# A norm factor computed two value groups sooner, and three weight splits moved behind a bank's read, in a two-layer hybrid decoder step on one Trainium2 core

## The chip, the core and the metric

The kernel runs on one core of a Trainium2 chip. Five engines work side by side, each through its own queue, in order: TensorE (PE; its weight loads are shown apart as PEld), VectorE (DVE), ScalarE (ACT), GpSimd (POOL) and SyncE (SP), which here issues all DMA transfers. An instruction that has to wait for another engine holds up everything behind it on its own engine. The metric is the device time of one execution in microseconds (us).

## The reference

There are 1088 tokens: 1024 of a prompt and 8 x 8 sample tokens. Layer 0 is a gated linear attention with 4 heads, layer 1 a token-mixing MLP on chunks of 128 positions. Cut to what the change touches:

```python
def gla_mixer(h, s0, w_in, ...):            # h = rmsnorm(x, norm_g[0])
    q, k, v, gate, a_low = split(h @ w_in)
    q = q * GLA_DK ** -0.5
    log_a = log_sigmoid(a_low @ w_a_up + b_a_up) / 16
    o, s_new = gla_chunked(q, k, v, log_a, s0, 64)
    return (rmsnorm(o, g_onorm) * silu(gate)) @ w_out, s_new

def cmlp_mixer(h, w_in, ...):               # h = rmsnorm(x, norm_g[1])
    u, v, gate = split(h @ w_in, 3)
    v = layernorm(v, ln_g, ln_b)
    mixed = einsum('gts,bnsgd->bntgd', tril(w_spatial), v) + b_spatial
    return (u * mixed * silu(gate)) @ w_out, v
```

## The kernel before

**Number format.** Matmuls run on operands split into a high part (the value rounded to the fast matmul format, a copy on ACT) and a low part (value minus high part, a subtraction on DVE). Each product is then three matmuls: high x high, high x low, low x high. So every weight tile that arrives costs one ACT and one DVE instruction before PE can use it: `fetch_w` (L127, L128) in most stages and `parts_of` (L972, L973) in the u/gate stage. Each tile here is 128 x 512 values.

**Start of layer 0.** The tokens lie in three pieces of 384, 384 and 320. The norm is applied late: matmuls run on x times the norm's gain, and the factor 1/rms of each token (`rs[p]`) is multiplied in when a result is read out. `squares_x(p)` sums x*x over the eight row blocks (ACT squares L236, DVE adds L238). `rstd_x(p)` sums over the partitions with a matmul of ones (L244, tile ssq) and makes the factor in two ACT steps (L179 logarithm, L181 exponential) and four DVE steps (L180, L182, L183, L184). `evac_qk` reads the queries and keys of a piece out of PSUM times that factor (L264, L266). `token_rstd` sends the factors through memory to lay them out by token (L190, L191, L194, tile rtm).

Queries and keys of head 0 are multiplied first, for all three pieces; the third piece's wait in two PSUM banks (tile third) for their factor. Then come the groups of values of head 0, `v_group(0, i)`, i = 0 to 8, one per 128 tokens, 24 matmuls each (L156), with 16 extra columns: the input of the forget gate (tile alt). Groups 0 to 4 (`AHEAD` = 5) run ahead of the attention's work. After group 3 (`LOW0` = 3) stand `a_low(0)`, which transposes the gate inputs of the first piece (L252) and splits them (L255, L256, L257), and `gates()` of the first piece: one matmul (L419), then L422 to L426 and a scan (L428) that gives the running sum of the log gates, cum. From cum come the attention's operands: `borders` (L435 to L449) and `level_prep` (L459 to L463, L470 to L483), on DVE, ACT and POOL, for the matmuls of `level` (L509, L518).

**What sets the order there.** Outside the u/gate stage, a planner orders the instructions of each engine when the kernel is built: it goes through them by its own estimate of when each is ready, and among those that are ready the earlier line of the program goes first. Moving a line changes its rank, and can change the order of others. The tiles' buffers are few: the tag misc, from which ssq, pa and z (the banks of the norm, the gate inputs and the gate matmul) come, has two PSUM banks.

**u/gate stage of layer 1.** From L1006 to L1267 the order is that of the program (`in_order`). The stage computes, for each of m = 0 to 7, 128 columns of u and of gate for all tokens. The 2 x 2 blocks of weights and tokens are combined so that seven products do the work of eight: the weights appear plain, (1,1), (1,2), (2,2), and as sums s1 to s4 made on POOL (`sums`, L985) out of the raw quarters (`Quarters`: four loads of 256 KB, L964, into one buffer, rawq). `parts(key, place)` splits one of them into a place (L972, L973); a place is free once the products that used the previous weights in it are done. `nxt` holds the weights of m + 1, `following` the loads for m + 2.

One m runs through products in this order, each for two halves r of 272 columns, 12 matmuls a half (L1004): s2 into the banks pb, s3 into two, s1 on pb, (1,1) into p, then the token mixing (L1106), s4 on pb, (2,2) on two, (1,2) on p. Between them: L1139 and L1179 copy halves out on ACT, L1165 adds pb to sg on DVE, L1191 and L1192 add halves on POOL, L1210 multiplies the norm factor on DVE and L1211 is the SiLU on ACT; L1218 reads pb for the last time on DVE, after which the next m's s2 product may write that bank; L1220 and L1222 multiply on POOL; L1240 reads two for the last time on DVE. `v_load(m + 1)` (L1076, L1077) loads the next values for mixing, normalised by L1083 on ACT.

For m = 0 the splits for m = 1 have an order of their own, since nothing was ready earlier. The lines are:

```python
for key, at in (((1, 1), "s2"), ((2, 2), "s3"), ((1, 2), "s1")):   # L1207
    nxt.parts(key, w[at])
following = Quarters(22)
V.tensor_tensor(sg[:, fb], sg[:, fb], rs_all[:, fb], ALU.mult)     # L1210
A.activation(sg[:, fb], sg[:, fb], AF.Silu)                        # L1211
nxt.parts("s2", spare)                                             # L1213
for r in R:
    product(pb[r], w["s4"], b22[r], start=False)                   # L1217
    V.tensor_tensor(p1[r], p1[r], pb[r], ALU.add)                  # L1218
    if r == 0:
        G.tensor_tensor(zt[:, qb[r]], zt[:, qb[r]], p1[r], ALU.mult)
```

Of the kernel before, what the change touches and what calls it, by code (L numbers as in the profile page):

```python
# [34 lines left out]
WARM, AHEAD, LOW0 = 9, 5, 3  # L35
# [5 lines left out]
def trunk_kernel(ctx: ExitStack, tc: tile.TileContext, a: dict):  # L41
# [28 lines left out]
    def ps(tag, name, bufs=2):  # L70
        return pp.tile([P, 512], F32, tag=tag, bufs=bufs, name=name)
# [114 lines left out]
    def token_rstd(p):  # L186

        t0, n, nch = PIECES[p]
        row = a["r_spill"]
        SP.dma_start(row[:, t0:t0 + n], rs[p][0:1, :])  # L190
        SP.dma_start(rtm[:, 3 * p:3 * p + nch], row[0, t0:t0 + nch * P].rearrange("(c q) -> q c", q=P))  # L191
        if p == 2:
            for r in (0, NS):
                SP.dma_start(rtm[r:r + NS, 8:9], row[0, SEQ:T].rearrange("(c q) -> q c", q=NS))  # L194
# [20 lines left out]
    def gq(tag, name, bufs):  # L215
        return gc.tile([P, NPMAX], F32, tag=tag, bufs=bufs, name=name)
# [24 lines left out]
    def rstd_x(p, acc, ms, t):  # L241
        n = size[p]
        ssq = ps("misc", "ssq")[:, :n]
        PE.matmul(ssq, ones, acc, start=True, stop=True)  # L244
        rstd(ssq, D, rs[p], ms[:, :n], t[:, :n])
# [15 lines left out]
    def evac_qk(h, p, j, acc):  # L261
        t = gq("qk"[j], "qk"[j] + f"{h}_{p}", 4)[:, :size[p]]
        if j == 0:
            V.scalar_tensor_tensor(t, acc, QSCALE, rs[p], ALU.mult, ALU.mult)  # L264
        else:
            V.tensor_tensor(t, acc, rs[p], ALU.mult)  # L266
        (q, k)[j][h, p] = t
# [13 lines left out]
    first = [ps("mm", f"first{j}")[:, :size[0]] for j in range(2)]  # L281
# [9 lines left out]
    for i, t in enumerate((lvmask, smask)):  # L291
        f = wp.tile([P, 512], F32, tag="raw", bufs=3, name="mask")[:, :448]
# [24 lines left out]
    third = [fm_block(ws_[0], j * P, h0[2], 2, wide[:, j, :]) for j in range(2)]  # L317
# [7 lines left out]
    acc2 = squares_x(2)  # L325
# [5 lines left out]
    def gt(tag, name, bufs, shape=(P, NPMAX)):  # L331
        into = gc if tag in ("v", "la", "e", "cum", "dec") else gp
        return into.tile(list(shape), F32, tag=tag, bufs=bufs, name=name)
# [405 lines left out]
    ahead = block_groups(1)  # L739
    for i, g in enumerate(ahead[:AHEAD]):  # L740
        g()
        if i == LOW0:
            a_low(0)
            flat[0].gates()
    rstd_x(2, acc2, *(gt("sq", f"sq{j}", 2) for j in range(2)))
    for j in range(2):
        evac_qk(0, 2, j, third[j])
    token_rstd(2)
    hs = side_by_side(h0[2], "hs0", gc)

    LEAD = 3
# [1 line left out]
    for h in range(HEADS):  # L753
# [18 lines left out]
        at = {}  # L772
# [11 lines left out]
    i = 0  # L784
# [224 lines left out]
    nxt = None  # L1009
    for blk in range(16, 20):  # L1010
        cs = slice((blk - 16) * 256, (blk - 15) * 256)
        for j, i in enumerate((4, 5, 6, 7, 8, 0, 1, 2, 3) if blk == 19 else range(9)):
# [24 lines left out]
            if (blk, j) == (18, 7):  # L1037
                nxt = Quarters(20)
# [85 lines left out]
    cur, nxt = nxt, None  # L1124
    for m in range(KT):
        w, g, more = cur.w, m // 2, m + 1 < KT
        first = m == 0
# [12 lines left out]
        if first:  # L1140
            for key in ("s4", (2, 2), (1, 2)):
                cur.parts(key)
            nxt, spare = Quarters(21), place()
# [36 lines left out]
        if mid:  # L1180
            if m + 2 < KT:
                following = Quarters(22 + m)
            else:
                stage = mp.tile([P, 5, N], F32, tag="rawq", name="zstage")
                SP.dma_start(stage, z_d[:, 0:5, 0:N])
                following = None
# [16 lines left out]
            mixed(zt, vm, g, m, bias, 4 * c)  # L1203
        if m == 1:
            nxt.parts("s3", w[1, 1])
        if first:
            for key, at in (((1, 1), "s2"), ((2, 2), "s3"), ((1, 2), "s1")):  # L1207
                nxt.parts(key, w[at])
            following = Quarters(22)
        V.tensor_tensor(sg[:, fb], sg[:, fb], rs_all[:, fb], ALU.mult)  # L1210
        A.activation(sg[:, fb], sg[:, fb], AF.Silu)  # L1211
        if first:
# [3 lines left out]
        for r in R:  # L1216
            product(pb[r], w["s4"], b22[r], start=False)  # L1217
            V.tensor_tensor(p1[r], p1[r], pb[r], ALU.add)  # L1218
            if r == 0:
                G.tensor_tensor(zt[:, qb[r]], zt[:, qb[r]], p1[r], ALU.mult)  # L1220
        mixed(zt, vm, g, m, bias, 0, True)
        G.tensor_tensor(zt[:, qb[1]], zt[:, qb[1]], p1[1], ALU.mult)  # L1222
        V.tensor_tensor(sg[:, fb], sg[:, fb], rs_all[:, fb], ALU.mult)
# [36 lines left out]
        if more:  # L1260
# [3 lines left out]
            cur, nxt = nxt, following  # L1264
# [144 lines left out]
```

## Time and profile before

| | |
|---|---|
| three runs | 935.84, 936.48, 936.76 us (median 936.48) |
| the profiled execution | 939.36 us, of which the span from first to last instruction is 937.6 us |
| busy over the span | PE 96%, PEld 94%, DVE 68%, ACT 49%, POOL 31% |
| mean granted TensorE clock | 0.994 |
| 40 to 60 us (value groups, first gates) | PE busy 18.15 of 20, DVE 13.82 |
| 60 to 80 us (first attention units) | PE busy 17.76 of 20, DVE 19.86 |
| 80 to 100 us | PE busy 20.00 of 20, DVE 14.00 |
| 640 to 660 us (m = 0 of u/gate) | PE busy 20.00 of 20, DVE 12.32, POOL 7.67 |
| 660 to 680 us (end of m = 0, m = 1) | PE busy 18.65 of 20, DVE 17.53, POOL 15.31 |
| 680 to 820 us (the other m) | PE busy 20.00 of every 20 |

How to read it: PE is busy nearly all the time, so a microsecond counts only where PE stands still, and the windows show where that is. In a row of the timeline stand the start, the duration, the engine, the line, the operation, the tiles out<-in, the shape and the count; in brackets the idle time before it and what ended it.

### The profile page before, as it was taken

Reading aid. Unit: us, or ns where it says so; the run is one execution under the profiler, and the core shown is the slowest. Engines: PE = TensorE matmul, PEld = TensorE weight load, DVE = VectorE, ACT = ScalarE, POOL = GpSimd, SP = SyncE. Lnnn points to the kernel's source line nnn. Section 1 sums busy time; section 2 is a strip of 40 time slices with the busy share of each in tenths; the row PEclk is TensorE's granted clock in tenths of the full one; section 3 lists DMA queues with packets and bytes.
Section 4 is the critical chain, followed back from the end, with each engine's and each line's share of the span. In section 5 each row is a group of like instructions: output and inputs, shape, how many; then the busy total and the mean of one; then the engine's idle time right before and its main releaser. Section 6 shows DMA issues by size and latency. Waiting matters only on the chain.

```text
span 937.6 us, 17096 instructions
## 1 busy us (share of the span) xinstructions
PE 904.3 (96%) x6437; PEld 877.5 (94%) x6437; DVE 638.7 (68%) x1288; ACT 461.4 (49%) x980; POOL 287.1 (31%) x307
## 2 busy tenths in 40 slices
PE   8989999999999999989999999999999999999995
PEld 7979989998999989989999999999999999999994
DVE  7888778677875877687653854556877777683246
ACT  7664544444552644554443644457444444465322
POOL 2023332332422332322134110021765555211123
PEclk9999999999999999999999999999999999999998
DMA  9302112301222112423565245554333332464233
GB/s 297 96 1 83 41 45 77 118 29 50 64 77 92 52 35 91 124 74 101 155 226 176 73 145 157 156 171 138 99 126 106 102 97 95 125 222 130 60 109 130
DMA packets 89968, 101.80 MB, mean 109 GB/s; under 512 B 9863, under 2 KB 80845, under 8 KB 89885
## 3 DMA queue, kind: packets, MB, share of 16 engines
q1 hardware_dynamic: 89884, 100.71, 34.4%
q8 instruction: 50, 0.82, 0.4%
q14 instruction: 34, 0.27, 0.1%
HBM read 74.26 MB, written 26.42 MB: 107 GB/s over the span
## 4 chain that ended last, share of the span: by engine, by line
PE 66%; DVE 15%; ACT 5%; DMA 5%; issue 5%; POOL 2%; SPq 1%; DVEq 0%; ACTq 0%; POOLq 0%
PE fm L142 27%; PE tm L156 12%; PE pb L1004 7%; PE two L1004 5%; PE p L1004 4%; DMA xsum<-x_spill 2%; PE sc L518 2%; PE mix L1106 1%; PE pst L589 1%; PE o L628 1%; PE o L597 1%; DVE scT L531 1%; DMA wr<-w 1%; PE o L599 1%; PE tms L172 1%
## 5 line engine op out<-in xcount | busy, mean ns | idle before, releaser
L142 PE MATMUL fm<-act,w 128*128 128x384 f32 (+1 forms) x1632 | 292.3, 334 | 0.5 <-DVE act L203 0.4
L142 PEld LDWEIGHTS fm<-act,w 128*128 128x128 f32 x1632 | 271.1, 189 | 3.2 <-DVE act L206 0.7
L156 PE MATMUL tm<-w,act 128*128 128x256 f32 (+1 forms) x1536 | 193.3, 283 | 1.4 <-ACT vt L1015 1.0
L156 PEld LDWEIGHTS tm<-w,act 128*128 128x128 f32 x1536 | 185.5, 188 | 3.7 <-ACT vt L1015 1.9
L142 PE MATMUL fm<-act,wq 128*128 128x384 f32 (+1 forms) x576 | 97.2, 328 | 1.3 <-ACT wq L127 0.8
L142 PEld LDWEIGHTS fm<-act,wq 128*128 128x128 f32 x576 | 94.7, 188 | 3.4 <-ACT wq L127 1.4
L128 DVE TENSOR_TENSOR w<-wr,w 128x512 fp32r<-128x512 f32 (+1 forms) x80 | 57.2, 732 | 17.4 <-ACT w L127 16.9
L826 POOL TENSOR_TENSOR acc<-acc,sq 128x384 f32<-128x384 f32 (+1 forms) x30 | 30.6, 1023 | 110.8 <-ACT sq L821 110.3
L127 ACT ACTIVATE w<-wr 128x512 fp32r<-128x512 f32 (+1 forms) x80 | 48.7, 625 | 25.2 <-DMA wr<-w 13.7
L848 DVE TENSOR_TENSOR x<-fm,res 128x384 f32<-128x384 f32 (+1 forms) x40 | 21.0, 527 | 50.5 <-PE fm L142 50.5
L1004 PE MATMUL two<-tsum,wq 128*128 128x272 f32 x384 | 51.5, 290 | 0.0
L1004 PE MATMUL pb<-act,wq 128*128 128x272 f32 x384 | 51.4, 290 | 0.0
L821 ACT ACTIVATE sq<-x 128x384 f32<-128x384 f32 (+1 forms) x42 | 21.0, 502 | 61.3 <-DVE x L848 58.3
L1004 PE MATMUL p<-act,wq 128*128 128x272 f32 x384 | 51.0, 289 | 0.0
L1004 PEld LDWEIGHTS p<-act,wq 128*128 128x128 f32 x384 | 49.4, 188 | 0.0
L1004 PEld LDWEIGHTS two<-tsum,wq 128*128 128x128 f32 x384 | 49.2, 189 | 0.0
L1004 PEld LDWEIGHTS pb<-act,wq 128*128 128x128 f32 x384 | 49.1, 189 | 0.0
L473 POOL TENSOR_TENSOR xe<-xe,k 128x384 f32<-128x384 f32 (+2 forms) x24 | 28.7, 1195 | 44.3 <-ACT xe L472 41.1
L659 POOL TENSOR_TENSOR on<-on,g 128x384 f32<-128x384 f32 (+1 forms) x24 | 23.8, 1015 | 57.9 <-DVE on L658 35.1
L449 POOL TENSOR_TENSOR kd<-kd,k 128x384 f32<-128x384 f32 (+1 forms) x12 | 12.0, 1003 | 85.7 <-ACT kd L448 85.7
L480 DVE TENSOR_TENSOR xl<-cum 128x192 f32<-128x192 f32 (+4 forms) x72 | 34.8, 509 | 0.0
L483 DVE TENSOR_TENSOR xl<-xl,q 128x192 f32<-128x192 f32 (+4 forms) x72 | 28.9, 439 | 4.8 <-ACT xl L481 4.8
(265 smaller groups left out, 1638.9 us busy)
## 6 DMA issues: line engine op xcount, KB each, us to landing
wr<-w SPq DMA_DIRECT2D x92, 256.0 KB, 3.1
rawq<-w SPq DMA_DIRECT2D x32, 256.0 KB, 3.6
xsum<-x_spill SPq DMA_DIRECT2D x16, 272.0 KB, 3.2
z_spill<-zt SPq DMA_DIRECT2D x8, 544.0 KB, 2.8
s<-s SPq DMA_DIRECT2D x16, 256.0 KB, 4.3
state_s<-ns SPq DMA_DIRECT2D x32, 128.0 KB, 1.8
v_spill<-vt SPq DMA_DIRECT2D x32, 128.0 KB, 2.5
vm<-v_spill SPq DMA_DIRECT2D x8, 512.0 KB, 4.7
```

The costliest lines, as they stand in the source:

```text
L127: A.activation(w[:, 0], raw, AF.Copy)
L128: V.tensor_tensor(w[:, 1], raw, w[:, 0].bitcast(F32), ALU.subtract)
L142: PE.matmul(acc, lhs, rhs, start=(k == 0), stop=(k == 23))
L156: PE.matmul(acc, lhs, rhs, start=(k == 0), stop=(k == 23))
L473: G.tensor_tensor(xe, xe, kt_[:, :nl], ALU.mult)
L480: V.tensor_tensor(l3[:, :, lo:hi], c3[:, :, (i + 1) * m:], r, ALU.subtract)
L483: V.tensor_tensor(l3[:, :, lo:hi], l3[:, :, lo:hi], q3[:, :, (i + 1) * m:], ALU.mult)
L659: G.tensor_tensor(o, o, gate[h][:, j, t0:t0 + n], ALU.mult)
L821: A.activation(sq, raw[p][:, m, :], AF.Square)
L826: (V if gain is not None and p == 2 or m == KT - 1 else G).tensor_tensor(total, acc[p], sq, ALU.add)
L848: V.tensor_tensor(raw[p][:, m, :], pa, r, ALU.add)
L1004: PE.matmul(acc, lhs, rhs, start=start and k + i == 0, stop=k + i == 5, skip_group_check=not start)
```

## The change

Two places are edited. In the start of layer 0, `rstd_x(2, ...)` moves from behind value group 4 to behind group 2, and the reading out of the third piece's queries and keys and `token_rstd(2)` move from behind group 4 to behind group 3, after the first piece's `gates()`. In the u/gate stage at m = 0, the plain splits (1,1) and (2,2) move from ahead of L1210 to behind the last read of pb's first half and the POOL multiplication of that half; the split (1,2) moves behind the last read of the second half; the loads for m = 2 come after it. No computation is added or removed.

```diff
     for i, g in enumerate(ahead[:AHEAD]):
         g()
+        if i == LOW0 - 1:
+            rstd_x(2, acc2, *(gt("sq", f"sq{j}", 2) for j in range(2)))
         if i == LOW0:
             a_low(0)
             flat[0].gates()
-    rstd_x(2, acc2, *(gt("sq", f"sq{j}", 2) for j in range(2)))
-    for j in range(2):
-        evac_qk(0, 2, j, third[j])
-    token_rstd(2)
+            for j in range(2):
+                evac_qk(0, 2, j, third[j])
+            token_rstd(2)
     hs = side_by_side(h0[2], "hs0", gc)
...
         if m == 1:
             nxt.parts("s3", w[1, 1])
-        if first:
-            for key, at in (((1, 1), "s2"), ((2, 2), "s3"), ((1, 2), "s1")):
-                nxt.parts(key, w[at])
-            following = Quarters(22)
         V.tensor_tensor(sg[:, fb], sg[:, fb], rs_all[:, fb], ALU.mult)
         A.activation(sg[:, fb], sg[:, fb], AF.Silu)
...
             V.tensor_tensor(p1[r], p1[r], pb[r], ALU.add)
             if r == 0:
                 G.tensor_tensor(zt[:, qb[r]], zt[:, qb[r]], p1[r], ALU.mult)
+            if first:
+                for key, at in ((((1, 1), "s2"), ((2, 2), "s3")), (((1, 2), "s1"),))[r]:
+                    nxt.parts(key, w[at])
+        if first:
+            following = Quarters(22)
         mixed(zt, vm, g, m, bias, 0, True)
```

## The prediction

> **What bounds the kernel now.** I read the windows first: the stretch of each edit, and what follows it.
>
> ```profile
> 53.00:79.10 26.10, 22.13 (x157) 19.76 (x155) 25.96 (x61) 16.84 (x40) 10.29 (x11) 1.00 0.04 7
> 79.10:99.90 20.80, 20.75 (x142) 20.27 (x143) 14.85 (x36) 7.87 (x19) 5.06 (x6) 1.00 0.28 86
> 663.20:667.70 4.50, 3.15 (x25) 3.12 (x25) 4.27 (x9) 1.75 (x4) 2.33 (x4) 1.00 0.64 201
> ```
>
> The columns are the stretch, its length, the busy time of PE, PEld, DVE, ACT and POOL, the granted clock, DMA share and GB/s. From 53.0 to 79.1 us DVE is busy 25.96 of 26.10 and PE stands still for 3.97: DVE sets the pace. Behind that PE is full again, so what PE gains in the stretch it keeps. Around 665 us PE loses 1.35 of 4.50. These two places are all that the edits can win.
>
> In the first place DVE's timeline shows it idle just before (start, duration, engine, line, operation, tiles; in brackets the idle time before it):
>
> ```profile
> 44.12 1.68 DVE L238 TENSOR_TENSOR acc<-acc,sq 128x320 f32<-128x320 f32 x3
> 48.09 0.55 DVE L256 TENSOR_TENSOR alow<-pa,alow 16x384 fp32r<-16x384 f32 x1 [2.28 <-ACT alow L255]
> 49.74 0.62 DVE L422 TENSOR_SCALAR la<-z,vecs 128x384 f32<-128x384 f32 x1 [1.11 <-PE z L419]
> 52.48 0.56 DVE L426 TENSOR_TENSOR la<-la,e 128x384 f32<-128x384 f32 x1 [2.12 <-ACT e L425]
> 52.96 0.48 DVE L180 TENSOR_SCALAR sq<-ssq 128x320 f32<-128x320 f32 x1
> 53.36 0.95 DVE L428 TENSOR_TENSOR_SCAN cum<-scan,la 128x384 f32<-128x384 uint8 x1
> ...
> 57.23 0.48 DVE L264 SCALAR_TENSOR_TENSOR q<-third,rs 128x320 f32<-128x320 f32 x1
> 57.63 0.48 DVE L266 TENSOR_TENSOR k<-third,rs 128x320 f32<-128x320 f32 x1
> ```
>
> The squares of the third piece are summed at 45.80 (44.12 + 1.68). Then DVE waits 2.28 + 1.11 + 2.12 = 5.5 us for the chain of the first gates, and only behind it come, among the operations that PE waits for, the six of the third piece: L180, L182, L183, L184, L264, L266.
>
> **The norm edit.** Nothing is added; six DVE, two ACT and two PE instructions move. On DVE each takes 0.40 of its queue (57.23 to 57.63), so 6 x 0.40 = 2.4 us leave the stretch in which DVE is the bound, and they fit into the idle 5.5. What they may delay there, in PE's and ACT's timelines:
>
> ```profile
> 37.24 9.78 PE L156 MATMUL tm<-w,act 128*128 128x272 f32 x76 [0.24 <-DVE w L128]
> ...
> 50.70 0.70 PE L244 MATMUL ssq<-acc,ones_r 128*128 128x320 f32 x2
> ...
> 59.30 0.53 PE L509 MATMUL sc<-x 128*64 128x64 f32 x6 [1.36 <-DVE x L463]
> ```
>
> ```profile
> 52.34 0.52 ACT L179 ACTIVATE sq<-ssq,vecs 128x320 f32<-128x320 f32 x1
> ```
>
> Value group 3 runs at 9.78/76 = 0.129 a matmul, 3.1 us for 24; the row ends at 47.02 with it, so it lies from about 43.8 to 46.9. The sum at 45.8 falls within it. The planner places by its own estimates, which the trace doesn't show; L238 stands in its orders close to where it ran, so I take the ssq matmuls in the middle of group 3, at 45.9. They put the rest back by some 0.3 (2 matmuls of 320 columns instead of 272). Then the ACT logarithm until about 47.1, L180 to 47.7, and L182 to L184 until about 48.9. L256, which would start at 48.09 + 0.3, stands behind these four: another 0.5. So the gate chain is 0.8 late; but L180 no longer stands between L426 and the scan (0.40 back). Net delay 0.4 to 0.5. Queries and keys go into the idle time ahead of L422 or L426 and cost nothing; without that cover, 0.8. Sum: 2.4 - 0.5 = **1.9 us** off at L463, which follows L266 and releases the first scores (59.30, after 1.36 of waiting). PE's 3.97 of standing still is more than 1.9, so PE can take all of it.
>
> Late next is still DVE, with cum's operations. The four DMA issues of `token_rstd` come earlier too, and with them the factors by which value groups 6 to 8 are read out; they pass no other transfer that this stretch waits for (its DMA share is 0.04). Of the two misc banks ssq now takes one ahead of pa and z; z comes after L180 has read it.
>
> Bounds: at worst the six stay on the chain all the same (work is only moved), 0; at best no delay, 2.4. I take 1.9, the row-by-row sum. The planner may order later units differently; the nearest row is the wait at 59.30, 1.36, either way.
>
> **The splits edit.** Here the program's order holds, so each queue can be followed. Before, on POOL and on DVE:
>
> ```profile
> 654.71 1.82 POOL L985 TENSOR_TENSOR qsum<-qsum,rawq 128x512 f32<-128x512 f32 x1
> 656.49 1.22 POOL L1191 TENSOR_TENSOR half<-half 128x272 f32<-128x272 f32 x1
> 657.67 1.22 POOL L1192 TENSOR_TENSOR sg<-sg,half 128x272 f32<-128x272 f32 x1
> 658.85 0.77 POOL L1191 TENSOR_TENSOR half<-half 128x272 f32<-128x272 f32 x1
> 659.59 0.77 POOL L1192 TENSOR_TENSOR sg<-sg,half 128x272 f32<-128x272 f32 x1
> 660.32 1.27 POOL L985 TENSOR_TENSOR qsum<-rawq 128x512 f32<-128x512 f32 x1
> ```
>
> ```profile
> 654.70 3.56 DVE L973 TENSOR_TENSOR wq<-rawq,wq 128x512 fp32r<-128x512 f32 x3
> 660.39 1.79 DVE L1210 TENSOR_TENSOR sg<-sg,rs 128x544 f32<-128x544 f32 x1 [2.13 <-POOL sg L1192]
> 663.43 0.69 DVE L973 TENSOR_TENSOR wq<-qsum,wq 128x512 fp32r<-128x512 f32 x1 [1.25 <-ACT wq L972]
> 664.04 0.78 DVE L1218 TENSOR_TENSOR half<-half,pb 128x272 f32<-128x272 f32 x2
> 664.73 0.28 DVE L1101 SCALAR_TENSOR_TENSOR zt<-mix,lng,bias 128x64 f32<-128x64 f32 x1
> 664.93 0.97 DVE L1223 TENSOR_TENSOR sg<-sg,rs 128x544 f32<-128x544 f32 x1
> 665.82 0.77 DVE L1240 TENSOR_TENSOR sg<-half,two 128x272 f32<-128x272 f32 x2
> 666.52 1.28 DVE L973 TENSOR_TENSOR wq<-qsum,wq 128x512 fp32r<-128x512 f32 x2
> ```
>
> While the three splits run (3.56 instead of about 3 x 0.60, the spacing of 663.43 to 664.04), POOL's additions are long too: 1.82 against 1.27, 1.22 twice against 0.77. DVE and POOL take turns, each waiting out the other's whole operation. L1210 (1.79) waits out the sum of 660.32 (1.27) the same way, and then has some 0.6 of its own. [...]
>
> What goes: with the splits gone, POOL's chain is 0.55 + 2 x 0.45 = 1.45 shorter, L1192 ends at 658.9 instead of 660.36, and L1210 (still 1.79), SiLU, the s2 split and L1218 of r = 0 follow 1.45 sooner: the first bank is free at about 663.0.
>
> ```profile
> 660.09 3.18 PE L1004 MATMUL p<-act,wq 128*128 128x272 f32 x24
> 664.61 3.26 PE L1004 MATMUL pb<-tsum,wq 128*128 128x272 f32 x24 [1.35 <-DVE half L1218]
> 667.71 3.18 PE L1004 MATMUL two<-tsum,wq 128*128 128x272 f32 x24
> 670.72 3.16 PE L1004 MATMUL pb<-act,wq 128*128 128x272 f32 x24
> ```
>
> PE ends p at 663.27, so the 1.35 wait before pb is gone. What comes in its place: behind L1218 of r = 0 DVE now has (1,1) (662.97), then L1220 takes its turn on POOL (the shape of L1192: 0.74 from start to start), then (2,2): L1218 of r = 1 ends at 665.2 and not 663.4. PE wants that bank 1.5 after 663.15, at 664.65, and gets it at 665.35: it waits 0.7. Then DVE has (1,2) 0.60, the sample mixing 0.20, L1223 0.60 (no longer blocked by L1220, as in its 0.97), L1240 0.70, s3 0.65: s3 is split at 667.95, before at about 667.2. PE wants two at 666.85, gets the bank at 667.5 and s3's low half at 668.0; from there 22 matmuls of 3.01/24 end at 670.8, against 670.72 before. So the waits move from one bank to the next three places: +0.1. The ACT copies, which DVE waits for (1.25 before 663.43), come in a row behind SiLU and stay ahead of DVE.
>
> The loads for m = 2 now wait for the (1,2) split and start at about 665.9 instead of 663.37; on SP the values for m = 1 stand behind them:
>
> ```profile
> 663.37 1.75 SPq L964 DMA_DIRECT2D rawq<-w  x4
> 665.17 0.43 SPq L1076 DMA_DIRECT2D vm<-v_spill  x1
> ```
>
> ```profile
> 670.72 1.65 ACT L1083 ACTIVATE vm<-vm,lt,lr 128x128 f32<-128x128 f32 x4
> ```
>
> ```profile
> vm<-v_spill SPq DMA_DIRECT2D x8, 512.0 KB, 4.7
> ```
>
> Their issue moves to about 667.7, and with 4.7 to landing (the page's DMA issues) they are there at 672.4, so L1083 starts 1.7 later and its first four end at 674.1. The mixing that reads them follows pb and p of m = 1 (two halves of 1.5 each) near 676.8; the five chunks behind the four come close to it. I put +0.1 on that: **+0.2** for this edit. Bounds: -1.35 (the whole wait goes) to +2.0 (below); I take the middle because DVE's queue up to s3 gains 1.45 and gets three splits of 0.60 and one turn of POOL.
>
> **Sum.** -1.9 + 0.2 = -1.7: the profiled 939.36 (span 937.6 and 1.8 around it) would be 937.7, the median 936.48 becomes **934.8 us**.
>
> **The rivals.** (1) PE waits for the sum. If the planner puts ssq at group 3's beginning, PE stands from 43.9 to 45.9 and everything behind is 2.2 later; the DVE work still leaves the later chain, so the edit keeps only about 0.5: 936.2. For it: the planner cannot see DMA waits on ACT and DVE. Against: the other waits in this stretch are short.
>
> (2) Both win. If (2,2) isn't held by L1220, 0.7 less falls on the second bank and on s3: the splits edit gives -0.6, and with 2.2 to 2.4 from the norm edit 933.6. The rows of turn-taking speak against it.
>
> (3) Slower. POOL's spans are rough. If L1192 ends at 660.36 as before, the three splits only lengthen DVE's queue between L1210 and s3, by 1.8 less idle: PE waits 1.5 us longer at two, and the values arriving behind the loads add up to 0.5 at the mixing. It decides by L1192's end: at 658.9 nothing is lost, each 0.1 later costs 0.1. With nothing from the norm edit: 936.48 + 2.0 = 938.5. Against: 1.22 beside 0.77 in one series.
>
> **Chances.** Forecast 0.45 (own range 934.0 to 935.6), (1) 0.22, (2) 0.20, (3) 0.10, other orders 0.03. The range 932.8 to 937.4 leaves out (3) and little else. 0.2% (1.9 us, limits 934.6 and 938.4) is about what a measurement can tell from no change. Faster: 0.20 of the forecast, (2), and 0.01: 0.41. Slower: 0.08 of (3) and 0.03: 0.11. Same: 0.48.
>
> **What would show it.** Norm edit: ssq near 45.9 and not 50.70, L264 and L266 ahead of the scan, the first scores near 57.4 and not 59.30, PE's idle in 53 to 79 falls from 3.97 to about 2; a PE wait before ssq shows (1). Splits edit: L1191 and L1192 all at 0.77, L1210 starts near 658.95, pb without its first wait but with one of 0.7 for its second half, two at 667.5, s1's pb again near 670.8 less the first edit's gain. Wrong it is if waits in the other units of attention (100 to 480 us) change by more than 1.4, or if the mixing at m = 1 waits.

## The result, and the profile after

The changed kernel takes 943.65 us in the median of seven executions (941.96 to 947.58), the kernel before 936.76 beside it (seven executions, 935.84 to 940.26). The ratio is 1.0069, with a 95% interval of 1.0052 to 1.0086: slower by some 6.5 us (the two medians lie 6.9 apart), where 934.8 was forecast and 932.8 to 937.4 was the range. Its profiled execution took 944.07 us, with a span of 942.3. Line numbers behind an edit shift a little: L1107, L1210 and L1218 of the kernel before are L1108, L1207 and L1215 in the changed kernel, and each kernel's rows carry its own numbers.

The windows of the changed kernel, in the columns that the prediction's first fence has:

```profile
53.00:79.10 26.10, 22.78 (x161) 21.31 (x160) 22.89 (x47) 17.98 (x43) 10.15 (x11) 0.93 0.04 13
79.10:99.90 20.80, 19.48 (x132) 18.73 (x131) 16.43 (x42) 7.01 (x16) 5.30 (x5) 1.00 0.28 77
663.20:667.70 4.50, 3.75 (x26) 3.34 (x26) 4.50 (x9) 1.88 (x4) 2.44 (x3) 1.00 0.19 47
```

In the window around 665 us PE stands still for 0.75 instead of 1.35; but a wait of 0.42 ends just before the window opens, at 663.17, so that it is 1.17 in all. DVE is busy 22.89 of 26.10 and not 25.96 in the first stretch: the 2.4 us of DVE work did leave it, and DVE is idle there for 3.2 us instead of 0.1. PE's granted clock is 0.93 there, and the stretch behind it is no longer full (19.48 of 20.80).

PE's timeline shows where the first chain of gates went:

```profile
46.13 0.81 PE L244 MATMUL ssq<-acc,ones_r 128*128 128x320 f32 x2 [1.09 <-DVE acc L238]
...
48.78 0.49 PE L252 MATMUL pa<-ident,alt 128*16 128x128 f32 x3
...
51.74 0.41 PE L419 MATMUL z<-alow,wup 128*128 128x384 f32 x1 [0.22 <-ACT alow L257]
...
59.74 0.53 PE L509 MATMUL sc<-x 128*64 128x64 f32 x6 [1.85 <-DVE x L463]
...
65.66 0.47 PE L419 MATMUL z<-alow,wup 128*128 128x384 f32 x1
```

The same transposes (L252) and the first z in PE's timeline of the kernel before:

```profile
46.86 0.49 PE L252 MATMUL pa<-ident,alt 128*16 128x128 f32 x3
...
49.29 0.41 PE L419 MATMUL z<-alow,wup 128*128 128x384 f32 x1
```

And DVE's timeline of the changed kernel:

```profile
47.53 0.49 DVE L180 TENSOR_SCALAR sq<-ssq 128x320 f32<-128x320 f32 x1 [1.46 <-ACT sq L179]
...
49.09 0.49 DVE L184 SCALAR_TENSOR_TENSOR rs<-sq,rs 128x320 f32<-128x320 f32 x1
49.62 0.49 DVE L264 SCALAR_TENSOR_TENSOR q<-third,rs 128x320 f32<-128x320 f32 x1
50.03 0.48 DVE L266 TENSOR_TENSOR k<-third,rs 128x320 f32<-128x320 f32 x1
50.54 0.55 DVE L256 TENSOR_TENSOR alow<-pa,alow 16x384 fp32r<-16x384 f32 x1
...
55.56 0.96 DVE L428 TENSOR_TENSOR_SCAN cum<-scan,la 128x384 f32<-128x384 uint8 x1
...
58.85 0.74 DVE L463 TENSOR_TENSOR x<-x,q 128x192 f32<-128x192 f32 x1
```

PE waits 1.09 for the sum of squares, and L256 has all six moved operations ahead of it, queries and keys too: it starts at 50.54 instead of 48.09, and z at 51.74 instead of 49.29. The first scores come at 59.74, not at the 57.4 of the forecast (59.30 before), and the second z at 65.66; in PE's timeline of the kernel before it is at 62.97.

In the u/gate stage PE's timeline shows m = 0 much as forecast, and m = 1 not:

```profile
639.08 3.58 PE L1005 MATMUL pb<-tsum,wq 128*128 128x272 f32 x24
...
663.17 1.74 PE L1005 MATMUL pb<-tsum,wq 128*128 128x272 f32 x12 [0.42 <-DVE half L1215]
665.21 1.77 PE L1005 MATMUL pb<-tsum,wq 128*128 128x272 f32 x12 [0.30 <-DVE half L1215]
667.43 3.54 PE L1005 MATMUL two<-tsum,wq 128*128 128x272 f32 x24 [0.45 <-DVE sg L1242]
670.80 3.22 PE L1005 MATMUL pb<-act,wq 128*128 128x272 f32 x24
...
679.32 3.27 PE L1005 MATMUL pb<-act,wq 128*128 128x272 f32 x24 [0.49 <-DVE sg L1166]
684.62 0.41 PE L1101 MATMUL mix<-wss,vm 128*128 128x64 f32 x2 [2.04 <-DVE zt L1108]
684.84 4.79 PE L1005 MATMUL two<-tsum,wq 128*128 128x272 f32 x24
...
692.48 3.17 PE L1005 MATMUL pb<-tsum,wq 128*128 128x272 f32 x24
```

The kernel before, for the same two ends (first products of m = 0 and of m = 2):

```profile
639.60 3.58 PE L1004 MATMUL pb<-tsum,wq 128*128 128x272 f32 x24
...
687.80 3.17 PE L1004 MATMUL pb<-tsum,wq 128*128 128x272 f32 x24
```

From m = 0 to m = 2 it takes 53.40 us (692.48 - 639.08) where before it took 48.20. Up to s1's pb it is 31.72 against 31.12 (670.72 - 639.60), so 0.6 is lost at m = 0 and 4.6 at m = 1. Of these 4.6, a wait of 2.04 stands ahead of the sample mixing, and the two product behind it takes 4.63 (to 689.47, where p begins) instead of 3.10 (684.78 - 681.68 in the timeline of before). Most of the rest is lost ahead of s4's pb, where PE waits 0.49 for DVE's L1166. The window of the changed kernel in which most of that product lies has a granted clock of 0.50, the third number from its end:

```profile
686.00:688.00 2.00, 2.00 (x11) 2.00 (x10) 2.00 (x5) 1.18 (x2) 1.21 (x2) 0.50 0.94 292
```

What PE waits for is DVE's L1108, and that is late because of a split ahead of it. DVE's queue and then POOL's, changed kernel:

```profile
679.53 3.68 DVE L974 TENSOR_TENSOR wq<-rawq,wq 128x512 fp32r<-128x512 f32 x1
683.13 0.68 DVE L974 TENSOR_TENSOR wq<-qsum,wq 128x512 fp32r<-128x512 f32 x1
683.73 1.40 DVE L1108 SCALAR_TENSOR_TENSOR zt<-mix,lng,bias 128x512 f32<-128x512 f32 x2
```

```profile
671.78 1.29 POOL L986 TENSOR_TENSOR qsum<-rawq 128x512 f32<-128x512 f32 x1 [4.31 <-DMA rawq<-w]
...
679.72 0.76 POOL L1192 TENSOR_TENSOR half<-half 128x272 f32<-128x272 f32 x1
680.45 0.76 POOL L1193 TENSOR_TENSOR sg<-sg,half 128x272 f32<-128x272 f32 x1
681.17 0.76 POOL L1192 TENSOR_TENSOR half<-half 128x272 f32<-128x272 f32 x1
681.90 0.76 POOL L1193 TENSOR_TENSOR sg<-sg,half 128x272 f32<-128x272 f32 x1
```

One split (the next, behind POOL's last addition, takes 0.68) takes 3.68: it ends at 683.21, when POOL has made all four of its additions (the last ends at 682.66). Before, POOL's sums for m = 2 began at 669.08 and not at 671.78. Its additions began at 677.88 and took turns with the splits (1.02, 1.22, 0.77 and 1.23 on POOL, 0.77 and 1.25 on DVE), and L1107 ran at 679.37. DVE's queue of the kernel before:

```profile
678.19 1.25 DVE L973 TENSOR_TENSOR wq<-qsum,wq 128x512 fp32r<-128x512 f32 x1
679.37 1.40 DVE L1107 SCALAR_TENSOR_TENSOR zt<-mix,lng,bias 128x512 f32<-128x512 f32 x2
```

### The profile page after: what moved, and what is told of

Its sections match the earlier page's. It is cut to its first block, busy times and chain, and to the rows that moved or that the text cites. A ratio compares the mean times of both kernels' runs of the same rounds, so it can differ in the third digit from the quotient of the medians.

```text
span 942.3 us, 17095 instructions
## 1 busy us (share of the span) xinstructions
PE 907.5 (96%) x6437; PEld 880.9 (93%) x6437; DVE 642.7 (68%) x1288; ACT 461.5 (49%) x980; POOL 284.7 (30%) x307
## 4 chain that ended last, share of the span: by engine, by line
PE 61%; DVE 16%; DMA 7%; ACT 6%; issue 5%; POOL 2%; SPq 1%; DVEq 0%; ACTq 0%; POOLq 0%
PE fm L142 26%; PE tm L156 9%; PE pb L1005 6%; PE two L1005 4%; PE p L1005 4%; DMA xsum<-x_spill 2%; PE sc L518 2%; DMA wr<-w 1%; PE pst L589 1%; DVE wq L974 1%; PE mix L1107 1%; PE o L628 1%; DMA xt<-x_spill 1%; PE o L597 1%; DVE xl L480 1%
## 5 line engine op out<-in xcount | busy, mean ns | idle before, releaser
L1005 PE MATMUL two<-tsum,wq 128*128 128x272 f32 x384 | 53.4, 296 | 0.5 <-DVE sg L1242 0.5
L449 POOL TENSOR_TENSOR kd<-kd,k 128x384 f32<-128x384 f32 (+1 forms) x12 | 12.2, 1015 | 83.1 <-ACT kd L448 83.1
L480 DVE TENSOR_TENSOR xl<-cum 128x192 f32<-128x192 f32 (+4 forms) x72 | 37.2, 542 | 0.0
```

Source lines behind the costliest of these rows:

```text
L480: V.tensor_tensor(l3[:, :, lo:hi], c3[:, :, (i + 1) * m:], r, ALU.subtract)
L1005: PE.matmul(acc, lhs, rhs, start=start and k + i == 0, stop=k + i == 5, skip_group_check=not start)
```

## The experiments

My first theory after the result, A in the expectations, was that the whole loss lies in the u/gate stage. The run of the norm edit alone refuted it, and two theories were left: the norm edit loses at the first chain of gates, through the order that the planner made of it (call it O); the splits edit loses at m = 1, because the loads for m = 2 come late, and with them POOL's sums, which then keep DVE from its splits ahead of the mixing (call it L). Rivals are named in the expectations. The numbers of all runs come first; "m = 0 to m = 2" is the time between the first products of the two, in the one execution that was profiled. Each ratio is to executions of the kernel before that were taken with that run; their medians went from 936.76 to 940.05, so the medians of two rows are not to be compared, only the ratios.

| kernel | median us (executions) | ratio to before, 95% interval | first z | m = 0 to m = 2 |
|---|---|---|---|---|
| before, profile shown above | | | 49.29 | 48.20 |
| after | 943.65 (7) | 1.0069 (1.0052 to 1.0086) | 51.74 | 53.40 |
| n1_norm_alone | 941.36 (12) | 1.0039 (1.0021 to 1.0058) | 50.95 | 48.21 |
| s1_splits_alone | 940.86 (11) | 1.0036 (1.0020 to 1.0053) | 49.38 | 48.93 |
| s5_late_loads_only | 942.27 (6) | 1.0044 (1.0025 to 1.0063) | 49.48 | 51.70 |
| s3_last_split_only | 940.75 (7) | 1.0030 (1.0012 to 1.0047) | 49.10 | 52.38 |
| n2_one_group | 940.40 (12) | 1.0012 (0.9994 to 1.0030) | 49.11 | 50.76 |
| n3_factor_only | 942.04 (12) | 1.0034 (1.0018 to 1.0050) | 51.03 | 48.22 |
| s4_sums_behind | 941.94 (12) | 1.0027 (1.0004 to 1.0050) | 49.01 | 50.49 |
| s6_values_first | 942.20 (12) | 1.0036 (1.0019 to 1.0052) | 48.68 | 52.66 |
| b0_before_again | 939.14 (11) | 0.9988 (0.9976 to 0.9999) | 48.75 | 48.20 |
| s7_behind_factor | 939.40 (12) | 1.0001 (0.9985 to 1.0018) | 49.06 | 48.45 |
| s8_mixing_first | 938.97 (11) | 0.9990 (0.9976 to 1.0004) | 49.34 | 48.61 |
| a1_change_mixing_first | 940.97 (9) | 1.0037 (1.0020 to 1.0053) | 51.08 | 48.85 |

**Each edit alone.** The norm edit without the splits edit, and the reverse.

```diff
 n1_norm_alone: the change's first hunk only
 s1_splits_alone: the change's second and third hunks only
```

> The norm edit alone. Theory A (the loss lies in the u/gate stage): the span up to the first product of m = 0 is about 0.5 us shorter, as in the changed kernel's trace (639.08 instead of 639.60), and the whole is 0 to 1 us faster than before. Rival (the new order of the attention units also costs, in runs other than the profiled one): 1 us or more slower.

> The splits edit alone. Theory A: it carries the loss, 5 to 7 us slower; PE waits about 2 us for L1107 ahead of m = 1's sample mixing, and the granted clock halves behind it. Rival: under 2 us slower, the rest of the loss being in the norm edit.

Both lose, 0.39% and 0.36%; their product, 1.0075, is the whole change's 1.0069 within the intervals. In the norm edit alone the first z comes 1.66 late, and the u/gate stage is as before (48.21). In the nine profiles whose code is the same up to there (before, b0 and all the s kernels) the first z lies between 48.68 and 49.48, so a single difference is good to some 0.8; the four kernels with the factor two groups sooner, at 50.95 to 51.74, are well outside. The splits edit alone lost only 0.73 from m = 0 to m = 2 in the execution that was profiled, which is the lowest of its eleven: there the long split (2.54) fell behind L1107 and cost nothing. The changed kernel has the same code there, and in its execution it fell ahead. What the other ten executions did is not shown.

**The late loads alone.** The splits stay where they were before; only the loads for m = 2 are held back, by a small read of the raw quarters on DVE behind L1223, so that they start at about 665.5.

```diff
 for key, at in (((1, 1), "s2"), ((2, 2), "s3"), ((1, 2), "s1")):
     nxt.parts(key, w[at])
-following = Quarters(22)
...
 V.tensor_tensor(sg[:, fb], sg[:, fb], rs_all[:, fb], ALU.mult)
+if first:
+    probe = up.tile([P, 4, 1], F32, tag="probe", name="probe")
+    V.tensor_copy(probe, nxt.rw[:, :, 1, :1])
+    following = Quarters(22)
```

> The kernel before, its splits left where they were; only a small read of the raw quarters is put behind L1223, so that the four loads for m = 2, and m = 1's values behind them on SP, start near 665.9 as in the changed kernel. Theory L (the late loads are the cause): PE's first wait of 1.35 stays, and m = 1's sample mixing waits as in the changed kernel; 4 to 7 us slower. Rival Q (the three splits later in DVE's queue are the cause): within 0.5 us of before.

Its loads start at 665.46. DVE, and then PE:

```profile
679.20 3.83 DVE L973 TENSOR_TENSOR wq<-qsum,wq 128x512 fp32r<-128x512 f32 x1
682.95 1.40 DVE L1107 SCALAR_TENSOR_TENSOR zt<-mix,lng,bias 128x512 f32<-128x512 f32 x2
```

```profile
683.84 0.41 PE L1100 MATMUL mix<-wss,vm 128*128 128x64 f32 x2 [2.65 <-DVE zt L1107]
```

The late loads alone make the same wait, 2.65, by the same long split, and cost 0.44% (the read that holds them back takes DVE 0.74 in itself). The splits need not move at all for the loss: L holds.

**One split later.** (1,1) and (2,2) stay ahead of L1210; only (1,2) and the loads move behind L1218.

```diff
-for key, at in (((1, 1), "s2"), ((2, 2), "s3"), ((1, 2), "s1")):
+for key, at in (((1, 1), "s2"), ((2, 2), "s3")):
     nxt.parts(key, w[at])
-following = Quarters(22)
...
     G.tensor_tensor(zt[:, qb[r]], zt[:, qb[r]], p1[r], ALU.mult)
+if first:
+    nxt.parts((1, 2), w["s1"])
+    following = Quarters(22)
```

> Only the split (1,2), and the loads behind it, move behind pb's reads; (1,1) and (2,2) stay. Theory L: the loads still start about 2 us late (near 665.5), so 2 to 6 us slower. Rival Q: a third of the moved DVE work, so under 1 us slower, or up to 0.5 faster by POOL's shorter chain.

The first wait before pb fell from 1.35 to 0.56, but the wait at m = 1's sample mixing is there (2.87, behind a split of 3.83), and the two product behind it takes 4.78. What is gained at m = 0 is less than what the late loads cost.

**Values or raw quarters.** The splits edit, with the loads for m = 2 behind the load of m = 1's values.

```diff
-if first:
-    following = Quarters(22)
 mixed(zt, vm, g, m, bias, 0, True)
...
 if more:
     vm = v_load(m + 1)
+if first:
+    following = Quarters(22)
```

> The splits edit alone, but the loads for m=2 stand behind the load of the values for m=1, so that the values do not come late; the raw quarters still do. If the late values (L1084 at 673.3 instead of 670.7) make the wait at m=1's mixing: no such wait, m=0 to m=2 back to 47 to 48.3 us, ratio 0.999 to 1.000. If the late raw quarters do (POOL's sums for m=2, late, run into DVE's splits ahead of L1108, and ACT's (1,1) copy stands waiting ahead of L1084): values land early, but L1108 still ends late in most executions, m=0 to m=2 between 48.5 and 53.5 us, ratio 1.002 to 1.005.

The values are early now (their two loads are issued at 654.25 and 654.68 instead of 667.62 and 668.09), and still PE waits 2.04 at the sample mixing, behind a split of 3.68. So it isn't the values, as the prediction had feared, that hold up the mixing, but the raw quarters.

**POOL's sums behind its additions.** The kernel before, but for m = 0 the sums s1 and s2 stand behind L1191/L1192, so that these need not wait for the raw quarters.

```diff
-if first:
-    nxt.sums("s1")
-    nxt.sums("s2")
 for r in R:
     G.tensor_tensor(p6[r], p6[r], p1[r], ALU.add)
     G.tensor_tensor(sg[:, qb[r]], sg[:, qb[r]], p1[r], ALU.add)
 if first:
-    nxt.sums("s3")
+    for key in ("s1", "s2", "s3"):
+        nxt.sums(key)
     nxt.sums("s4", up)
```

> Kernel before, but on POOL the sums s1 and s2 for m=1, which wait for the raw quarters, stand behind the L1191/L1192 additions; splits and loads stay where they were. It asks what PE's 1.35 wait before pb hung on. Theory P (on POOL's additions standing behind the sums, as the prediction said): the additions run ahead of 653.3, L1210 no longer waits for POOL, the first wait before pb goes, loads for m=2 are not later than 663.4, the mixing at m=1 does not wait, first product of m=0 to that of m=2 takes 46.8 us instead of 48.2, ratio about 0.9986. Rival D (the s2 split waits for its sum instead, and DVE's three splits of rawq are blocked by POOL's sums): the wait stays between 0.7 and 1.5, ratio 0.9995 to 1.0005. In either case it should not be over 0.1% slower, since no load moves back.

Neither theory had it. POOL's additions were done by 656.78, but DVE's three splits now ran beside the last of them and the sums that followed:

```profile
656.02 0.76 POOL L1189 TENSOR_TENSOR sg<-sg,half 128x272 f32<-128x272 f32 x1
656.75 1.27 POOL L985 TENSOR_TENSOR qsum<-rawq 128x512 f32<-128x512 f32 x1
658.10 1.63 POOL L985 TENSOR_TENSOR qsum<-qsum,rawq 128x512 f32<-128x512 f32 x1
```

```profile
655.64 6.32 DVE L973 TENSOR_TENSOR wq<-rawq,wq 128x512 fp32r<-128x512 f32 x3
661.89 1.80 DVE L1208 TENSOR_TENSOR sg<-sg,rs 128x544 f32<-128x544 f32 x1
```

The splits took 6.32 instead of 3.56, the factor came at 661.89 instead of 660.39, and PE's wait before pb grew to 1.91. At m = 1 there is a wait of 0.93 at the sample mixing too, behind a split of 3.85, although the loads (663.14) were not late. So late loads are one way into that collision, and not the only one.

**A control.** The kernel before, unchanged.

> The kernel before, unchanged, as a control: seven edits in a row have come out 0.1 to 0.4% slower than it. If that is their doing, its ratio to itself is 1.000 with an interval that holds 1, and a second trace of it shows again no wait at m=1's mixing, 48.2 us from the first product of m=0 to that of m=2, and the first z near 49.3. If something in the comparison favours the kernel before, the ratio is 1.002 or more.

Its ratio to itself is 0.9988 (0.9976 to 0.9999), an interval that just misses 1, so the intervals may be a little too narrow. The losses of 0.3 to 0.4% above are the edits' own; but 0.1% is as near as these comparisons come.

**Two repairs of the splits edit.** In s7 all three splits and the loads stand between L1210 and the SiLU L1211. In s8 the splits edit is as in the change, but at m = 1 the split (1,2), the s2 split and the loads for m = 3 move behind the mixing, so that no split stands between L1165 and L1107.

```diff
 s7_behind_factor, against before
+V.tensor_tensor(sg[:, fb], sg[:, fb], rs_all[:, fb], ALU.mult)
 if first:
     for key, at in (((1, 1), "s2"), ((2, 2), "s3"), ((1, 2), "s1")):
         nxt.parts(key, w[at])
     following = Quarters(22)
-V.tensor_tensor(sg[:, fb], sg[:, fb], rs_all[:, fb], ALU.mult)
 A.activation(sg[:, fb], sg[:, fb], AF.Silu)
```

```diff
 s8_mixing_first, against s1_splits_alone
-        if mid:
+        if mid and m > 1:
             nxt.parts((1, 2), w["s1"])
             nxt.parts("s2", spare)
...
-        if mid:
+        if mid and m > 1:
             if m + 2 < KT:
                 following = Quarters(22 + m)
...
         for c in range(2):
             mixed(zt, vm, g, m, bias, 4 * c)
         if m == 1:
+            nxt.parts((1, 2), w["s1"])
+            nxt.parts("s2", spare)
+            following = Quarters(22 + m)
             nxt.parts("s3", w[1, 1])
```

> All three plain splits and the loads for m=2 stand one step later than before: behind the norm factor's multiplication (L1210) and ahead of the SiLU. POOL's additions are then clear of them, as after the change, but the loads are not late. Theory L (the splits edit lost only by the loads that it put back): the factor's multiplication ends near 660.7 as after the change, the splits follow by 662.6 while ACT does the SiLU, the first wait of 1.35 falls to 0.4 to 0.8, loads start by 664.0, no wait at the mixing of m=1, m=0 to m=2 in 47.3 to 48.0 us, ratio 0.999 to 1.0005. Rival C (what the splits cost is POOL's and DVE's sharing, wherever they stand): POOL's sums of s3 and s4 are stretched instead, loads at 664.5 or later, m=0 to m=2 49 us or more, ratio 1.001 to 1.004.

> The splits edit alone, and at m=1 the split (1,2), the s2 split and the loads for m=3 moved behind the two chunks of the mixing. Theory L's last link (DVE waits 3.7 us in a split behind POOL's four additions, ahead of L1108, and PE waits for L1108): with the split behind L1108 PE does not wait at m=1's sample mixing although the loads for m=2 are as late as before (rawq at about 665.8, vm landing late), m=0 to m=2 in 47.3 to 48.5 us, ratio 0.9985 to 1.001. If the late values themselves hold the mixing up, a wait of 1 us or more stays there. Rival: the loads for m=3, now late too, move the wait to m=2: m=0 to m=2 short, but a wait of 1 to 3 us between 700 and 710 us.

In s8 the loads are as late as after the change (665.73), and the long split is there, now behind L1107. DVE, and then PE:

```profile
679.00 1.40 DVE L1107 SCALAR_TENSOR_TENSOR zt<-mix,lng,bias 128x512 f32<-128x512 f32 x2
680.32 2.36 DVE L973 TENSOR_TENSOR wq<-rawq,wq 128x512 fp32r<-128x512 f32 x1
```

```profile
681.90 0.33 PE L1100 MATMUL mix<-wss,vm 128*128 128x64 f32 x2
```

PE's timeline marks no wait, there or later up to 740 us, and the ratio goes from 1.0036 to 0.9990 (0.9976 to 1.0004). This is the last link of L, and it is shown. But even so the edit wins nothing: 48.61 from m = 0 to m = 2, since waits of 0.29 and 0.45 at m = 0 and a slower two product (3.54 against 3.18) took the place of the wait of 1.35, much as the prediction said, and some 0.3 more goes ahead of s4's pb at m = 1. In s7 the loads came at 664.14, nothing waits at the mixing, and the ratio is 1.0001; but the wait before pb is 1.59, since the splits now met POOL's s3 and s4 sums and took 2.98. What the splits edit moves is a meeting of DVE and POOL, and in these runs each place had its own.

**The norm edit in smaller steps.** In n2 all of it stands one group sooner than before, behind group 3's `gates()`; in n3 only `rstd_x` is moved, as in the change, and the reading out stays behind group 4.

```diff
 n2_one_group
         if i == LOW0:
             a_low(0)
             flat[0].gates()
+            rstd_x(2, acc2, *(gt("sq", f"sq{j}", 2) for j in range(2)))
+            for j in range(2):
+                evac_qk(0, 2, j, third[j])
+            token_rstd(2)
-    rstd_x(2, acc2, *(gt("sq", f"sq{j}", 2) for j in range(2)))
-    for j in range(2):
-        evac_qk(0, 2, j, third[j])
-    token_rstd(2)
```

```diff
 n3_factor_only
         g()
+        if i == LOW0 - 1:
+            rstd_x(2, acc2, *(gt("sq", f"sq{j}", 2) for j in range(2)))
...
-    rstd_x(2, acc2, *(gt("sq", f"sq{j}", 2) for j in range(2)))
```

> The norm edit one group sooner only: factor, reading out and its spreading all behind value group 3's a_low and gates instead of behind group 4. Theory O (the loss of the norm edit is made by the order in which the first chain of gates runs: PE's wait of 1.09 for the sum and DVE's q and k ahead of L256): here ssq stands behind pa and z, so PE does not wait for the sum, L256 stays near 48.1 and the first z near 49.3 (after the whole norm edit 51.7). Then PE at the second head's z is within 0.5 us of the kernel before, and the ratio 0.998 to 1.0005. Rival G (any sooner place of the six DVE operations costs, since they stand ahead of the gates' work on DVE): z near 49.3 but the scan late by 1 to 2 us, later z late by 1 us or more, ratio 1.001 to 1.003. Rival N (my prediction's gain is real once PE does not wait): -1.9 us, 0.998.

> Only rstd_x(2) goes two groups sooner; the reading out of queries and keys and token_rstd stay behind group 4. Separates the two delays of the norm edit: PE's wait for the sum (1.09 in the changed kernel) and DVE's L264, L266 ahead of L256. Theory O with both parts: PE's wait of about 1.1 stays, L256 at about 49.7 instead of 50.54, first z near 50.9, later z late by 1.0 to 1.5 us, ratio 1.001 to 1.003. If the wait for the sum is all of it: first z still near 51.7 and ratio as the norm edit alone, 1.004. If q and k are all of it: first z near 49.5, ratio 0.999 to 1.000.

In n3 the planner placed L264 and L266 ahead of L256 all the same (DVE's timeline: L264 at 48.91, L256 at 49.83), though they stand two groups further down in the program: they were ready. It told the two delays of z apart no better than n1, and lost the same, 0.34%. In n2 z is on time (49.11), and the loss is 0.12% (-0.06 to 0.30). (Its 50.76 from m = 0 to m = 2 is not the edit's: the code there is the one before, and the pb product behind a wait of 1.97 fell on a clock of 0.57, from 668 to 672 us.) Its DVE and PE show why nothing is won then either:

```profile
53.82 0.95 DVE L428 TENSOR_TENSOR_SCAN cum<-scan,la 128x384 f32<-128x384 uint8 x1
54.69 0.46 DVE L266 TENSOR_TENSOR k<-third,rs 128x320 f32<-128x320 f32 x1
...
55.60 1.37 DVE L441 TENSOR_TENSOR kd<-cum 128x384 f32<-128x384 f32 x1
56.90 0.94 DVE L470 TENSOR_TENSOR xe<-cum 128x384 f32<-128x384 f32 x1
57.76 1.15 DVE L463 TENSOR_TENSOR x<-x,q 128x192 f32<-128x192 f32 x1
```

```profile
59.05 0.53 PE L509 MATMUL sc<-x 128*64 128x64 f32 x6 [2.14 <-DVE x L463]
```

Five of the six operations are ahead of the scan, and L463 still starts only 0.27 sooner than before (57.76 against 58.03), of which 0.18 is the sooner z of this execution. Two things eat the gain. The scan starts 0.46 later (53.82 against 53.36): on ACT the factor's L179 and L181 now run between the gates' own steps, and L264 goes ahead of the scan. And behind the scan 1.6 us of work (four operations) are gone, but only 0.73 of time: L441 takes 1.37 instead of 0.55, L470 0.94 instead of 0.55, beside POOL's L436 (55.41 to 56.56) and L462 (56.52 to 57.42). PE, meanwhile, did its filler products sooner and then waited 2.14 for the first scores instead of 1.36.

**Both, with the repair.** The whole change with s8's edit at m = 1.

> The whole change with the same repair at m=1 (split (1,2), s2 split and the loads for m=3 behind the mixing). If the two edits lose by two separate mechanisms, what is left is the norm edit's loss: first z near 51.7, m=0 to m=2 in 47.3 to 48.8 us without a wait at m=1's sample mixing, ratio 1.002 to 1.004 (the norm edit alone was 1.0039, the splits edit so repaired 0.9990, the whole change 1.0069). If the edits act on each other (the u/gate loss needs the late start of it, or the norm loss is a matter of the clock), the ratio stays at 1.005 to 1.007, or falls to 1.000.

The ratio is 1.0037 (1.0020 to 1.0053), that of the norm edit alone. The first z is at 51.08, nothing waits at m = 1's sample mixing, and m = 0 to m = 2 takes 48.85. The repair at m = 1 takes the one loss away and leaves the other: they come from two places.

## Why the prediction was wrong

**The norm edit, -1.9 forecast; about +1.9 at one clock, +3.7 in the median.** Three steps of it failed, and its sum counts L180 twice: the 2.4 already holds its 0.40, and the "0.40 back" takes it off again. By its own rows it should have read 2.4 - 0.8 = 1.6.

First, the place of the ssq matmuls, "in the middle of group 3, at 45.9", without a wait. They came at 46.13, but behind 1.09 of PE standing still: the planner placed them ahead of what PE could have done meanwhile. The prediction put the rest of PE's row back by "some 0.3"; the transposes came 1.92 later (48.78 against 46.86), by the wait of 1.09, 0.40 for the two matmuls and 0.43 that no row explains. ACT's L255, on which L256 hangs, came 1.92 later with them (49.51 against 47.59). In the four kernels with the factor two groups sooner the first z comes 5.60 to 5.61 behind ssq, whatever the wait ahead of it (0.46 in n3 to 1.09): the gates now hang on the sum. That was rival (1), with a smaller wait than its 2.2 and with a delay that was not given back later.

Second, the delay of L256, "another 0.5". L180 started at 47.53 and not 47.2, the four operations of the factor, each waiting for the last, stand 0.52 apart and not 0.40 (47.53 to 49.09), and the queries and keys, which the prediction had put "into the idle time ahead of L422 or L426", went ahead of L256: 0.92 more. L256 came 2.45 late, and not 0.8; since L255 had come 1.92 late, only some 0.5 of that is DVE's queue. The prediction had seen that a moved line changes its rank, and priced that for later units only; the first to be reordered were the lines next to it. In n3, where L264 and L266 stand two groups further down, they went ahead all the same, so it was readiness and not the place of the line that decided.

Third, the gain itself: "6 x 0.40 = 2.4 us leave the stretch in which DVE is the bound". DVE was busy for 25.96 of 26.10 us there, but a part of this was longer instructions beside POOL's: L460 1.17 while POOL's L436 ran (54.95 to 56.23) and L463 1.13 while its L449 ran (57.95 to 58.94), where the same lines take 0.34 and 0.35 later, with no POOL row beside them. L463 twice in DVE's timeline of the kernel before:

```profile
58.03 1.13 DVE L463 TENSOR_TENSOR x<-x,q 128x192 f32<-128x192 f32 x1
...
63.62 0.35 DVE L463 TENSOR_TENSOR x<-x,q 128x192 f32<-128x192 f32 x1
```

n2 takes four of the five behind the scan out with z on time, and L463 gains 0.27 at most, since the scan came later, L463 took 1.15 again, and L441 (1.37) and L470 (0.94) were the long ones in L460's place. In the changed kernel the scan comes 2.20 late (55.56 against 53.36) and L463 0.82, so 1.38 of the 2.0 us that left the queue behind the scan was won back, and the late gates took more than that.

What the delay is worth at the end: it stays through the attention stage. At the last z, near 400 us, the norm edit alone is 1.78 behind the kernel before (400.84 against 399.06), the whole change 2.58. The four kernels with the factor two groups sooner lie between 400.83 and 401.64 there, the nine with the code of before between 398.25 and 399.45; the means differ by 2.2, and by 2.1 at the first z. In the profiled execution of the norm edit alone it then vanishes, at least in part by the clock. PE behind a wait of 1.14 near 420 us, kernel before, then the norm edit alone:

```profile
420.38 4.18 PE L142 MATMUL fm<-act,w 128*128 128x384 f32 x14
```

```profile
421.43 2.64 PE L142 MATMUL fm<-act,w 128*128 128x384 f32 x14
```

The same 14 matmuls take 4.18 in the one and 2.64 in the other; the window from 422 to 424 us has a granted clock of 0.50 and 1.00. The profiled execution of the norm edit alone was the lowest of its twelve (938.56, clock 0.996). If the executions of equal mean clock are set against each other, over all those of the kernel before, the norm edit alone is 1.9 us slower, n3 1.5, n2 0.5, the splits edit alone 2.9, s8 0.2, s7 0.4, a1 2.4 and the whole change 3.1: an estimate, from means of few executions each. The control b0 comes out 0.5 slower than its own code by this reckoning, so 0.5 and less is nothing; the 1.9 agrees with the delay at the last z. That the losses add is shown by the medians alone: at one clock 1.9 and 2.9 would make 4.8 and not 3.1. What is left of the medians' differences goes with lower clocks: 0.9916 in the mean of the changed kernel's seven, 0.9932 to 0.9946 in four sets of the kernel before. Why the mean clock of its executions is lower was not tried, and so half of the norm edit's 3.7 has no shown cause; it has the longer waits.

**The splits edit, +0.2 forecast; +3.4 measured** (0.36% of 939). At m = 0 the working held. POOL's additions all took 0.76 to 0.78, L1207 started at 658.94 (658.95 forecast), the two product at 667.43 (667.5), s1's pb at 670.80 (670.8). The wait before pb's second half was 0.30 and not 0.7, and the one before its first half did not go altogether (0.42): the additions start behind the sums, which wait for the raw quarters, and these landed at about 653.3 as before, though PE began m = 0 0.52 sooner in this execution. So that the times agree to 0.1 is partly luck: counted from m = 0's first product, s1's pb came at 31.72 and not at 31.20. In s8, where PE began at 639.55, the first wait is not there, and s1's pb comes at 31.16.

What failed is "I put +0.1 on that", the late loads. The prediction followed the values through SP's queue to ACT, and found them near enough to the mixing; it named "the mixing at m = 1 waits" as what would make it wrong. It didn't follow the raw quarters, which are 2.5 us late as well, on to POOL's sums (the four end at 678.36, before at 675.72), and POOL's late row on to DVE's splits. s5, s6 and s8 show this chain from its two ends: late loads alone make the wait, values that come early don't take it away, and a mixing ahead of the splits does. The size failed with it: even rival (3) gave the mixing no more than 0.5, and the wait of 2.04 together with the slow product behind it (4.63 instead of 3.10) is 3.6 in the changed kernel.

**"DVE and POOL take turns"** was read from one place (654.7 to 658.9) and carried over to all. The traces here show both cases: alternation there (DVE's splits took 0.68, 1.78 and 1.25, POOL's sum 1.82 and its two additions 1.22 each, and from 655.38 to 658.89 their ends alternate), and a DVE split that ends behind four POOL operations in a row, 3.68 us in the changed kernel and 3.83 in s5 (in s3, s4 and s6 the split ahead of L1107 took 3.83, 3.85 and 3.68). The long split's row starts at 679.53 and the first addition's at 679.72, so which of the two starts first does not explain it.

None of the kernels beats the one before by more than these comparisons can tell; s8 at 0.9990 is nearest, and the kernel before against itself gave 0.9988.

## What to carry to other kernels

When an edit delays a load, follow the load's buffer through every engine that reads it, and each engine's late row on to the rows of other engines that grow longer beside it, not only the load next in the queue (here POOL's sums ended 2.6 us later, and a DVE split of 0.68 took 3.68). An engine's busy time can depend on what another does: here part of what was taken out of DVE's queue came back as longer instructions beside POOL's (in n2 L441 1.37 instead of 0.55), so look for the same shape at two durations before pricing work that leaves. And where a planner orders by readiness, work that is moved ahead competes first with its new neighbours, so the chain next to it is the one to price.

## What the runs showed of the hardware

- Where DVE's and POOL's instructions met, they were not lengthened evenly. A DVE split, 0.68 elsewhere, took 3.68, 3.68, 3.83, 3.83 and 3.85 us (after, s6, s5, s3, s4); in the changed kernel and in s5 POOL made four additions of 0.75 or 0.76 each meanwhile, so those were not lengthened. In the kernel before, at 656.49 and 657.67, the same additions took 1.22 each, beside splits of 1.78 and 1.25, and the next two, with no split beside them, 0.77 (658.85 and 659.59). What decides between the two was not found.
- PE's granted clock stood at half behind some of its waits, and not behind others as long. The two product took 4.79 behind a wait of 2.04 in the changed kernel (clock 0.50 from 686 to 688 us), 4.78 behind 2.87 in s3 (0.52 from 684 to 686), and 3.25 behind 2.65 in s5 (1.00 from 684 to 688); near 420 us the same wait of 1.14 was followed by 0.50 in the kernel before and by 1.00 in n1 (422 to 424). What sets it off was not found. At two of these places it cost 1.5 us each (4.79 against 3.27, 4.18 against 2.64), as much as the waits that the two edits were about.
